# A grouped norm whose roots enter as factors per token in the projection's sums

## The chip, the core and the metric

The kernel runs on one core of a Trainium2 chip. Its time is the device time of one execution in microseconds. Before the change the runs took 817.53 us (median of 3, 816.61 to 818.11).

A core has five engines that work side by side and meet through semaphores. TensorE (PE in the profile, its weight loads PEld) multiplies matrices out of SBUF into the eight banks of PSUM. VectorE (DVE) and ScalarE (ACT) work element by element on SBUF and PSUM. GpSimd (POOL) works on SBUF, and SyncE (SP) issues the loads. Each engine takes its own instructions in a fixed order.

## The reference, cut to what matters

Two layers, 256 tokens, width 1024, all float32. In each layer three branches (a Mamba-2 scan, a sliding-window attention, a forgetting attention) are fed by one input projection, gated, projected, and merged. The scan branch ends in a norm over four groups of 256 channels, and then comes its projection:

```python
def grouped_rms_norm(y, w, groups):
    b, s, d = y.shape
    yf = y.astype(jnp.float32).reshape(b, s, groups, d // groups)
    yf = yf * lax.rsqrt(jnp.mean(yf * yf, axis=-1, keepdims=True) + NORM_EPS)
    return (yf.reshape(b, s, d) * w.astype(jnp.float32)).astype(y.dtype)

# mamba2_branch ends in:
    y = y.reshape(b, s, SSM_INNER) * jax.nn.silu(z)
    return grouped_rms_norm(y, norm_w, SSM_GROUPS)

# and in each layer:
        ys = jnp.stack([y_a, y_b, y_c], axis=2)
        branch = jnp.einsum('bsiw,iwd->bsid', ys, w_proj[layer])
        g = jax.nn.sigmoid(gates.reshape(b, s, N_BRANCH, d) + gate_bias[layer])
        merged = jnp.sum(g * branch, axis=2)
        x = x + jnp.einsum('bsd,de->bse', merged, w_out[layer])
```

For each token and each group there is one root. It multiplies 256 channels of that token, and all of them lie in the sum over `w` of the projection. So a root can be applied before the projection, to each channel, or behind it, to the part of the sum that belongs to its group.

## The kernel before

**Precision.** A float32 operand is split into a high part, rounded to the format that TensorE takes at full rate (fp32r), and the low rest. A product of two operands is three matmuls, high by high, low by high and high by low. `split` (L288) makes the two parts: ScalarE rounds (`hi`, L291) and VectorE subtracts (`lo`, L292).

**Weights.** They come in by DMA as raw parts of 512 KB, six buffers, and are split into `hi` and `lo` parts of 128x1024, six buffers each. A piece of 512 output columns has four parts, each with two of the eight blocks of 128 input channels (`k`). `feed` (L384) issues the next split when a part is given back by `release` (L404), behind the last matmul that reads it. A piece is worked on once for each of the two token blocks of 128 (`t`), so its parts are given back in the second token block.

**Order.** TensorE's order is written out by the program: `ops` is a list of pieces of weights with the work on each. Smaller steps (the attentions, the scan, the norm) are generators started by `launch` (L113) with a due time in a clock that counts matmul time. `pump` (L148), called within and after the pieces, enters those that are due; `drain` (L163) forces all steps with a given number. `finish` (L847) hangs queued work of the other engines (`ends_later`) behind a given instruction of ScalarE. The order of VectorE, ScalarE and POOL is laid out by the planner that compiles the program, by program order, readiness and the buffers that are free; `high_priority` puts instructions ahead.

**The scan branch's end** in each layer is this list: four pieces of 256 columns for the gate path (`u_z` with `br == 0`, two channel blocks `u` of 128 each), two gate pieces of 512 of the scan branch, one gate piece of the third branch, then the projection of the scan branch in two pieces of 512, then the rest of the third branch.

`u_z` multiplies the scan's output `y.xs` by the gate path (`normed`), squares it on ScalarE and adds the squares of two blocks, which make a group. `group_norm` (L953) is launched for each of the four groups. It sums the squares over the channels by matmuls against ones, so that each token is a partition (L955). POOL takes the power -1/2 (L961), and VectorE refines it by a Newton step (L966 to L969). The roots must then multiply a layout in which channels are partitions and tokens run along a row. So a root's high and low parts are put on diagonals of 128x128 (ScalarE, L976), and a matmul of a matrix of ones by the diagonals copies them to all partitions (two matmuls of 256 columns into PSUM). VectorE multiplies `y.xs`, the norm's weight and this broadcast (L989), and the result is split into `y.yh[0]` and `y.yl[0]`, the left operands of the projection.

**The projection** of the first piece is `u_proj2` with `tok2`: two PSUM banks, one for each token block, and the halves of `k` in turn (t0, t1, t0, t1). The second piece is `u_proj`, one token block after the other, 24 matmuls into one bank. `merge` (L1111) multiplies the gate and the bank's sum (VectorE, L1118) and adds to the merged sums on POOL (L1119).

**PSUM** has three banks tagged "mm" (`pmm`) for dense products and five tagged "mx" (`pmx`) for everything else. Other buffers that the change touches: `L1` (14, one row of 256 floats), `L2` (8, 512 floats) and `L8` (6, 2048 floats).

Of the kernel before, what the change touches and what calls it, by code (L numbers as in the profile page):

```python
# [11 lines left out]
F32 = mybir.dt.float32  # L12
F32R = mybir.dt.float32r
# [35 lines left out]
def hybrid_trunk(  # L49
# [17 lines left out]
    def T(tag, shape, dtype=F32, bufs=None):  # L67
        count[0] += 1
        return sb.tile(shape, dtype, tag=tag, name=f"{tag}_{count[0]}",
                       bufs=bufs if bufs is not None else BUFS.get(tag, 1))  # L70
# [8 lines left out]
    def pmx():  # L79
        return PS("mx", 5)  # L80
# [20 lines left out]
    def mm(o, a, b, **kw):  # L101
        n = b.free_size()
        if a.dtype == F32R:
            clock["t"] += max(0.094, n / 2350.0)
        else:
            clock["t"] += max(0.2, n / 587.0) * (0.5 if a.free_size() == 64 or a.shape[0] == 32 else 1.0)
        nc.tensor.matmul(o, a, b, **kw)  # L107
# [5 lines left out]
    def launch(br, gen, delay=0.0):  # L113
        clock["n"] += 1
        waiting.append([clock["t"] + delay, clock["n"], br, gen, None, False])
# [32 lines left out]
    def pump(budget=BUDGET):  # L148
        t0 = clock["t"]
        half = False  # L150
        while True:
            over = clock["t"] - t0 >= budget
            if over and not half:
                return
            for m in sorted(waiting, key=lambda m: (m[0], m[1])):
                if ready(m) and (m[5] if over else not early(m)):
                    half = m[5]
                    enter(m)
                    break
            else:  # L160
                return

    def drain(br):  # L163

        left = 0
        while any(m[2] == br for m in waiting):
            for m in sorted(waiting, key=lambda m: (m[0], m[1])):
                if m[2] == br and allowed(m):
                    left += 1
                    enter(m)  # L170
                    break
            else:
                m = min((m for m in waiting if allowed(m)), key=lambda m: (m[0], m[1]))
                left += 1
                enter(m)
        if left and VERBOSE:
            print("drained", br, left, "at", round(clock["t"], 1))
# [103 lines left out]
    def halves(ap):  # L281

        return ap.rearrange("p (a i) -> p a i", a=2)
# [4 lines left out]
    def split(hi, lo, src, scale=None, keep=lambda f: f):  # L288

        if scale is None:  # L290
            keep(act)(hi, src, AF.Copy)  # L291
            keep(tt)(lo, src, hi.bitcast(F32), op=ALU.subtract)  # L292
        else:
            keep(act)(hi, src, AF.Copy, scale=scale)
            keep(stt)(lo, src, scale, hi.bitcast(F32), op0=ALU.mult, op1=ALU.subtract)
# [618 lines left out]
    def u_z(y, br, u, c):  # L914
        def f(w):
            if u == 0 and br != 0:
                y.sz[br] = T("L8", [P, NK, S])
            elif u == 0:
                y.yh[br] = T("L8", [P, 2, NK, P], F32R)
                y.yl[br] = T("L8", [P, 2, NK, P], F32R)  # L920
            o = T("L1", [P, S]) if br == 0 else y.sz[br][:, u, :]

            def gated():
                th = T("L1", [P, S])
                act(th, o, AF.Tanh, scale=0.5)  # L925
                stt(o, th, 1.0, o, op0=ALU.add, op1=ALU.mult)
                y.zdone.add((br, u))
            if br == 1:
                dma_sum(y, w, c, o)
                after_evictions(3, gated)  # L930
                pump()
                return
            chan_sum(y, w, c, o)

            def normed():
                gated()
                tt(y.xs[:, u, :], y.xs[:, u, :], o, op=ALU.mult)
                sq = T("L1", [P, S])
                act(sq, y.xs[:, u, :], AF.Square)
                y.sq.append(sq)  # L940
                if u % 2 == 1:
                    tt(y.sq[-2], y.sq[-2], y.sq[-1], op=ALU.add)
                    launch(3 if u < 4 else 4, group_norm(y, u // 2, y.sq[-2]), D_GN1)
            if br == 0:
                drain(0)

                ends_later.append(normed)
            else:
                gated()
            pump()  # L950
        return f

    def group_norm(y, g, q0):  # L953
        p = pmx()
        for t in range(2):  # L955
            mm(p[:, 2 * t:2 * t + 2], q0[:, t * P:(t + 1) * P], ones[:, 0:2], start=True, stop=True)
        v = T("sm", [P, 8])
        ts(v[:, 0:4], p[:, 0:4], 1.0 / 256, 4 * EPS, op0=ALU.mult, op1=ALU.add)  # L958

        r0 = T("sm", [P, 8])  # L960
        nc.gpsimd.tensor_tensor(r0[:, 0:4], v[:, 0:4], mhalf[:, 0:4], op=ALU.pow)  # L961
        rbs = [T("L1", [P, S], F32R) for _ in range(2)]

        def diagonals():
            a = T("sm", [P, 8])
            tt(a[:, 0:4], r0[:, 0:4], v[:, 0:4], op=ALU.mult)  # L966
            tt(a[:, 0:4], a[:, 0:4], r0[:, 0:4], op=ALU.mult)
            r = T("rs", [P, 8], bufs=4)
            stt(r[:, 0:4], a[:, 0:4], -3.0, r0[:, 0:4], op0=ALU.add, op1=ALU.mult)  # L969

            rh, rl = T("sm", [P, 8], F32R), T("sm", [P, 8])
            nc.vector.tensor_copy(rh[:, 0:4], r[:, 0:4])
            tt(rl[:, 0:4], r[:, 0:4], rh[:, 0:4].bitcast(F32), op=ALU.subtract)
            for rb, v_ in zip(rbs, (rh.bitcast(F32), rl)):
                for t in range(2):
                    act(rb[:, t * P:(t + 1) * P], ident, AF.Copy, scale=v_[:, 2 * t:2 * t + 1])  # L976


        ends_later.append(diagonals)
        yield D_GN2  # L980
        if diagonals in ends_later:
            ends_later.remove(diagonals)
            diagonals()
        p = pmx()
        for i, rb in enumerate(rbs):
            mm(p[:, 0:S], onesr, rb, start=(i == 0), stop=(i == 1))
        for u in (2 * g, 2 * g + 1):
            n = T("L1", [P, S])
            stt(n, y.xs[:, u, :], y.vec[:, 80 + u:81 + u], p[:, 0:S], op0=ALU.mult, op1=ALU.mult)  # L989
            split(y.yh[0][:, :, u, :], y.yl[0][:, :, u, :], halves(n))  # L990


    def u_cv(y, c, t, i=None):
# [85 lines left out]
    def u_proj(y, br, c, t):  # L1079
        def f(w):  # L1080
            if c == 0 and t == 0:
                drain(3 if br == 0 else br)
                if br == 1:
                    y.mg = T("L8", [P, 2, D])
                if br == 2:
                    y.mh = T("L8", [P, 2, NK, P], F32R)
                    y.ml = T("L8", [P, 2, NK, P], F32R)
            final = br == 2 and c > 0 and t == 1
            if final:

                j = stream.index((pieces_out[y.l], 0)) + 2
                limit(j, False)
            merge(y, br, c, t, tok(y.yh[br], y.yl[br], w, t), pin if final else lambda f: f)
            if final:
                limit(j + 1, True)
            pump()
        return f

    def u_proj2(y, br):

        def f(w):
            def late():
                drain(4)
                pump()
            drain(3)
            for t, p in enumerate(tok2(y.yh[br], y.yl[br], w, (pump, late, pump, lambda: None))):
                merge(y, br, 0, t, p)
            pump()
        return f

# [137 lines left out]
    for y in layers:  # L1248
# [27 lines left out]
        def gates_proj(br):  # L1276
            def g(b):
                c = 512 * b
                op(cols(C_G + D * br + c, 512), u_gate(y, br, c, 0), u_gate(y, br, c, 1))

            def p(b):
                c = 512 * b
                if b == 0 and br != 0:
                    op(None, lambda y=y: split_late(y, br))
                i = sub([(0, w_proj[l, br, :, c:c + 512])], 512)
                if b == 0 and br == 0:
                    op(i, u_proj2(y, br))
                else:
                    op(i, u_proj(y, br, c, 0), u_proj(y, br, c, 1))
            seq = [(g, 0), (p, 0), (g, 1), (p, 1)]  # L1290
            if br == 1 and l == 0:

                seq = [(g, 0), (g, 1), (p, 0), (p, 1)]
            if br == 0:

                seq = [(lambda b: z1(C_ZA, 0, b), b) for b in range(4)] + [(g, 0), (g, 1), (p, 0), (p, 1)]
            return [lambda f=f, b=b: f(b) for f, b in seq]
# [265 lines left out]
```

## Time and profile before

| | before |
|---|---|
| median of 3 runs | 817.53 us (816.61 to 818.11) |
| the profiled execution | 816.47 us, span 814.7 us |
| granted TensorE clock | 0.999 |
| TensorE, weight loads | 805.0 us, 717.2 us busy |
| VectorE, ScalarE, GpSimd | 675.2, 538.2, 162.6 us busy |
| HBM read | 154.63 MB, 192 GB/s over the span |

The span runs from the first to the last instruction of one execution. A row of the profile names engine, line, operation and tiles as "written<-read". L107 is the helper that issues every matmul, so its rows are told apart by tiles: `mm` and `mx` are the PSUM banks, `hi` and `lo` the weight parts, `L` any of the buffers `L1` to `L16`. "x4" counts instructions. A piece of the chain in order of time has a start, a length and what it was; an idle time in square brackets names what ended it. In the rows of matmuls the duration is that of a pipelined instruction, and the distance between two starts is what each costs.

### The profile page before, as it was taken

How to read it: one execution, taken by the hardware profiler on the slowest of the kernel's cores; microseconds unless marked ns; L12 is line 12 of the kernel's file. 1: busy time of each engine (PE TensorE's matmuls, PEld its weight loads, DVE VectorE, ACT ScalarE, POOL GpSimd, SP SyncE). 2: the span in 40 equal slices, each digit the busy share in tenths (PEclk: the TensorE clock that was granted, in tenths of full speed). 3: DMA queues.
4: the chain of work that ended last, by engine and by line, in shares of the span. 5: the costliest groups of instructions: out<-in, count | busy, mean ns of one | idle time of the engine just before them, and what ended most of it. 6: DMA issues, size and time to landing. Idle time of an engine off the chain costs nothing.

```text
span 814.7 us, 14971 instructions
## 1 busy us (share of the span) xinstructions
PE 805.0 (99%) x5198; PEld 717.2 (88%) x5198; DVE 675.2 (83%) x1452; ACT 538.2 (66%) x1168; POOL 162.6 (20%) x233
## 2 busy tenths in 40 slices
PE   9999999999999999999999999999999999999996
PEld 8998988888888988888999898888888889888896
DVE  6878899989998788865776989997989878787665
ACT  7777768865776768543666776885557767674452
POOL 3066113130310111130005711313002110102100
PEclk9999999999999999999999999999999999999999
DMA  9898787687865554866789878768877565467632
GB/s 316 279 258 197 220 225 203 195 251 227 234 208 181 156 165 146 270 200 205 235 261 265 198 219 226 198 199 237 247 234 205 153 190 169 133 210 261 206 104 77
DMA packets 138708, 170.35 MB, mean 209 GB/s; under 512 B 9346, under 2 KB 106362, under 8 KB 138634
## 3 DMA queue, kind: packets, MB, share of 16 engines
q1 hardware_dynamic: 114960, 140.53, 54.6%
q0 software_dynamic: 12928, 12.63, 9.6%
q10 hardware_dynamic: 10746, 16.24, 6.6%
q8 instruction: 41, 0.67, 0.3%
q14 instruction: 33, 0.27, 0.1%
HBM read 154.63 MB, written 2.16 MB: 192 GB/s over the span
## 4 chain that ended last, share of the span: by engine, by line
PE 81%; DVE 10%; DMA 3%; ACT 3%; issue 3%; ACTq 0%; DVEq 0%
PE mm L107 72%; PE mx L107 6%; PE mx L111 3%; DVE lo L292 3%; DMA L<-cumd 3%; DVE L L830 2%; ACT hi L291 1%; ACT pp L614 0%; DVE L L292 0%; ACT L L827 0%; DVE pp L643 0%; DVE L L894 0%; DMA L<-in_x_dram 0%; DVE pp L619 0%; DVE L L679 0%
## 5 line engine op out<-in xcount | busy, mean ns | idle before, releaser
L107 PE MATMUL mm<-L,hi 128*128 128x512 f32 x1056 | 355.3, 387 | 1.0 <-ACT qt L491 0.7
L292 DVE TENSOR_TENSOR lo<-raw,hi 128x1024 fp32r<-128x1024 f32 (+2 forms) x276 | 312.5, 1151 | 51.1 <-ACT hi L291 48.3
L107 PE MATMUL mm<-hi,L 128*128 128x512 f32 (+2 forms) x1232 | 322.9, 351 | 0.1
L291 ACT ACTIVATE hi<-raw 128x1024 fp32r<-128x1024 f32 (+2 forms) x276 | 265.0, 980 | 59.0 <-PE mm L107 49.3
L107 PE MATMUL mm<-L,lo 128*128 128x256 f32 x1056 | 266.6, 273 | 0.0
L107 PEld LDWEIGHTS mm<-hi,L 128*128 128x128 f32 x1232 | 217.3, 190 | 24.1 <-issue 1.3
L107 PEld LDWEIGHTS mm<-L,hi 128*128 128x128 f32 x1056 | 195.2, 190 | 29.0 <-issue 3.7
L107 PE MATMUL mm<-lo,L 128*128 128x512 f32 (+2 forms) x616 | 213.6, 348 | 0.0
L107 PEld LDWEIGHTS mm<-L,lo 128*128 128x128 f32 x1056 | 202.1, 191 | 5.2
L107 PEld LDWEIGHTS mm<-lo,L 128*128 128x128 f32 x616 | 116.3, 190 | 11.6
L492 POOL DMA_DIRECT2D L<-L x68 | 59.4, 885 | 193.0 <-ACT L L491 130.0
L830 DVE SCALAR_TENSOR_TENSOR L<-L,vec,L 128x255 f32<-128x255 f32 (+2 forms) x96 | 46.2, 481 | 1.7
L490 ACT ACTIVATE L<-mm 128x256 f32<-128x256 f32 x84 | 31.7, 378 | 21.0 <-PE mm L107 19.0
L1040 POOL TENSOR_SCALAR_AFFINE_SELECT bias<-bias 128x128 f32<-128x128 f32 x64 | 27.1, 459 | 87.1 <-DMA bias<-cumd 87.0
L1074 ACT ACTIVATE L<-L 128x512 f32<-128x512 f32 x24 | 15.1, 630 | 30.4 <-DVE L L1071 26.0
L656 ACT ACTIVATE pp<-pp,nm 128x128 f32<-128x128 f32 x64 | 28.2, 441 | 9.9 <-DVE nm L650 9.9
L492 POOL DMA_DIRECT2D qt<-L x16 | 13.8, 860 | 88.8 <-ACT qt L491 43.3
L614 ACT ACTIVATE pp<-pp,nm 128x128 f32<-128x128 f32 x32 | 12.6, 394 | 23.5 <-DVE nm L619 22.7
L961 POOL TENSOR_TENSOR sm<-sm,mhalf 128x4 f32<-128x4 f32 x8 | 9.9, 1240 | 88.2 <-DVE sm L958 88.2
L925 ACT ACTIVATE L<-L 128x256 f32<-128x256 f32 x48 | 19.8, 412 | 10.2 <-DVE L L483 10.0
L491 ACT ACTIVATE L<-mm 128x256 f32<-128x256 f32 x68 | 25.9, 381 | 0.7 <-DMA L<-L 0.7
L1119 POOL TENSOR_TENSOR L<-L,L 128x512 f32<-128x512 f32 x8 | 12.8, 1595 | 67.1 <-DVE L L1118 67.1
(210 smaller groups left out, 872.7 us busy)
## 6 DMA issues: line engine op xcount, KB each, us to landing
raw<-in_w_in_dram SPq DMA_DIRECT2D x191, 512.0 KB, 4.8
raw<-in_w_proj_dram SPq DMA_DIRECT2D x48, 512.0 KB, 5.4
L<-L POOLq DMA_DIRECT2D x72, 128.0 KB, 4.8
raw<-in_w_out_dram SPq DMA_DIRECT2D x16, 512.0 KB, 5.0
bias<-cumd ACTq DMA_DIRECT2D x16, 256.0 KB, 3.4
L<-cumd ACTq DMA_DIRECT2D x8, 512.0 KB, 6.0
L<-in_gate_bias_dram ACTq DMA_DIRECT2D x12, 256.0 KB, 5.0
qt<-L POOLq DMA_DIRECT2D x16, 128.0 KB, 5.5
```

The lines of the kernel that those rows point to most:

```text
L107: nc.tensor.matmul(o, a, b, **kw)
L111: nc.tensor.transpose(o, a, i)
L291: keep(act)(hi, src, AF.Copy)
L292: keep(tt)(lo, src, hi.bitcast(F32), op=ALU.subtract)
L490: act(halves(lo), ordered(p[:, S:2 * S]), AF.Copy)
L491: last = act(halves(out), ordered(p[:, 0:S]), AF.Copy)
L492: nc.gpsimd.dma_start(out, lo, accum_op=ALU.add)
L656: act(pp[:, i, sl], pp[:, i, sl], AF.Exp, scale=-1.0, bias=nm[:, e:e + 1], accum_out=sums[:, e:e + 1])
L830: stt(a[:, s:S], x_[:, 0:S - s], y.vec[:, 16 * j + u:16 * j + u + 1], a[:, s:S], op0=ALU.mult, op1=ALU.add)
L925: act(th, o, AF.Tanh, scale=0.5)
L1040: nc.gpsimd.affine_select(out=bias[:, i, dst], in_=bias[:, i, src], compare_op=ALU.is_ge, fill=NEG, base=0, pattern=[[-1, P]], channel_mul ...
L1074: finish(act(g, g, AF.Tanh, scale=0.5))
```

## The change

The roots are no longer applied to the channels. In `u_z` each block is split as soon as it is gated, with the norm's weight as the factor and without the root. The four groups' sums of squares are taken in one step (`group_norms`), launched after the last block: eight matmuls against ones into one bank, one evaluation and one power for all eight columns (group by token block), and one Newton step, queued in `ends_later`. The roots stay as they come, one token per partition.

Both projection pieces go through `u_proj_normed`: for each token block four sums of six matmuls, one per group, in banks taken in turn from "mm" and "mx". ScalarE copies the first with the root as its scale, and VectorE multiplies each of the other three by its root and adds. The merge then reads the result from SBUF. The diagonals, the broadcast matmuls and the multiplication by the broadcast go. `u_proj2` goes with them.

```diff
@@ u_z
             def normed():
                 gated()
                 tt(y.xs[:, u, :], y.xs[:, u, :], o, op=ALU.mult)
+                split(y.yh[0][:, :, u, :], y.yl[0][:, :, u, :], halves(y.xs[:, u, :]), scale=y.vec[:, 80 + u:81 + u])
                 sq = T("L1", [P, S])
                 act(sq, y.xs[:, u, :], AF.Square)
                 y.sq.append(sq)
                 if u % 2 == 1:
                     tt(y.sq[-2], y.sq[-2], y.sq[-1], op=ALU.add)
-                    launch(3 if u < 4 else 4, group_norm(y, u // 2, y.sq[-2]), D_GN1)
+                if u == NK - 1:
+                    launch(3, group_norms(y, y.sq[0::2]), D_GN1)
...
-    def group_norm(y, g, q0):
...
+    def group_norms(y, squares):
         p = pmx()
+        for g, q in enumerate(squares):
+            for t in range(2):
+                c = 4 * g + 2 * t
+                mm(p[:, c:c + 2], q[:, t * P:(t + 1) * P], ones[:, 0:2], start=True, stop=True)
+        v, r0 = T("sm", [P, 8]), T("sm", [P, 8])
+        ts(v, p[:, 0:16].rearrange("p (g i) -> p g i", i=2)[:, :, 0], 1.0 / 256, 4 * EPS, op0=ALU.mult, op1=ALU.add)
+        gtt(r0, v, mhalf, op=ALU.pow)
+
+        def newton():
+            y.roots = T("rs", [P, 8], bufs=4)
+            tt(v, r0, v, op=ALU.mult)
+            tt(v, v, r0, op=ALU.mult)
+            stt(y.roots, v, -3.0, r0, op0=ALU.add, op1=ALU.mult)
+
+        ends_later.append(newton)
+        yield 0.0
+
+    def u_proj_normed(y, c, t):
+        def f(w):
+            if c == 0 and t == 0:
+                drain(3)
+                for _ in range(len(ends_later)):
+                    ends_later.pop(0)()
+            acc = T("L2", [P, 512])
+            for g in range(4):
+                p = (pmx if g % 2 else pmm)()
+                for k in (2 * g, 2 * g + 1):
+                    for i, (a, b) in enumerate(((y.yh[0], w.hi), (y.yl[0], w.hi), (y.yh[0], w.lo))):
+                        mm(p, a[:, t, k, :], in_turn(b(k)), start=(k == 2 * g and i == 0),
+                           stop=(k == 2 * g + 1 and i == 2))
+                    if w.last and (k + 1) % w.kper == 0:
+                        release(w, k // w.kper + 1)
+                r = y.roots[:, 2 * g + t:2 * g + t + 1]
+                with tc.high_priority():
+                    if g == 0:
+                        act(acc, p, AF.Copy, scale=r)
+                    else:
+                        stt(acc, p, r, acc, op0=ALU.mult, op1=ALU.add)
+                if g == 1:
+                    pump()
+            merge(y, 0, c, t, ordered(acc))
+            pump()
+        return f
...
-    def u_proj2(y, br):
...
@@ gates_proj
-                if b == 0 and br == 0:
-                    op(i, u_proj2(y, br))
+                if br == 0:
+                    op(i, u_proj_normed(y, c, 0), u_proj_normed(y, c, 1))
```

More of the change, by code (lines that the diff above doesn't have):

```diff
@@ L951, in u_z @@
         return f
-    def group_norm(y, g, q0):
+    def group_norms(y, squares):
         p = pmx()
[L955 to L990, printed above, removed]
@@ L1081, in f @@
             if c == 0 and t == 0:
-                drain(3 if br == 0 else br)
+                drain(br)
                 if br == 1:
@@ L1095, in f @@
                 limit(j + 1, True)
-            pump()
-        return f
-    def u_proj2(y, br):
[L1101 to L1107, printed above, removed]
             pump()
```

## The prediction

> **What bounds the kernel now.** I read the page first: shares of the engines, and the chain that ended last.
>
> ```profile
> PE 805.0 (99%) x5198; PEld 717.2 (88%) x5198; DVE 675.2 (83%) x1452; ACT 538.2 (66%) x1168; POOL 162.6 (20%) x233
> ...
> PE 81%; DVE 10%; DMA 3%; ACT 3%; issue 3%; ACTq 0%; DVEq 0%
> ```
>
> TensorE is busy almost throughout and holds 81% of the chain; a fifth of the chain is elsewhere. So the stretch that the change touches has to be read alone. The chain in order of time shows it, first for layer 1 and then for layer 0 (start, length, what):
>
> ```profile
> 706.26 0.24 PE mx L107 x2
> 706.50 7.77 PE mm L107 x36
> 714.27 0.34 PE mx L107 x4
> 714.61 2.70 PE mm L107 x12
> 717.31 0.47 PE mx L107 x4
> 717.78 10.36 PE mm L107 x48
> 728.14 0.23 PE mx L107 x2
> 728.37 31.73 PE mm L107 x147
> ```
>
> ```profile
> 305.02 0.68 PE mx L107 x6
> 305.71 5.18 PE mm L107 x24
> 310.89 0.24 PE mx L107 x2
> ...
> 319.35 0.24 PE mx L107 x2
> ...
> 329.94 0.24 PE mx L107 x2
> ```
>
> The reader is to see that nothing but TensorE stands in the chain here: each piece starts where the one before it ends. The "mx" pieces are the norm's own: x4 are the sums of squares of a group (four matmuls against ones), x2 the broadcast of its roots. 48 large matmuls take 10.36 us, 0.216 each: one piece of 512 columns, two token blocks. The table by stage shows who stands behind TensorE (columns: PE, weight loads, DVE, ACT, POOL, each busy us and count, then granted clock, DMA share, GB/s). The four stretches are gates and projection of the scan branch in layer 0, then in layer 1:
>
> ```profile
> 296.00:332.00 36.00, 36.00 (x199) 31.19 (x197) 28.45 (x60) 26.84 (x53) 3.87 (x3) 1.00 0.58 176
> 332.00:353.00 21.00, 21.00 (x99) 18.40 (x98) 15.91 (x19) 8.97 (x10) 4.69 (x3) 1.00 0.71 219
> 700.00:733.00 33.00, 33.00 (x163) 29.19 (x164) 27.22 (x61) 23.52 (x47) 3.00 (x3) 1.00 0.55 168
> 733.00:754.00 21.00, 21.00 (x99) 18.40 (x98) 15.31 (x17) 10.21 (x11) 4.67 (x3) 1.00 0.77 259
> ```
>
> The clock is full, VectorE has 5 to 8 us free in each stretch. A microsecond of matmul taken out here comes off the end, as long as VectorE and ScalarE go on delivering the split weights in time.
>
> **What TensorE loses.** Per group two broadcast matmuls go, 16 in all. Their steps in the chain: 0.24 + 0.47 (two pairs) + 0.23 = 0.94 us in layer 1; in layer 0 three of 0.24, and of the x6 piece what is over the 0.34 of a x4 piece, 0.34: 1.06. Sum 2.0 us. The timeline gives the same for one pair by its starts: 310.96 - 310.72 = 0.24.
>
> ```profile
> 310.72 0.40 PE L107 MATMUL mx<-L,ones 128*128 128x256 f32 x2
> 310.96 0.60 PE L107 MATMUL mm<-hi,L 128*128 128x512 f32 x2
> ```
>
> The sums of squares stay 32 matmuls, but in one block per layer instead of four. What that is worth lies between 0.5 us saved and 0.5 us lost (a quarter of 0.34 for each of the six blocks that no longer stand apart); I take 0, since the nearest row is the same matmul. The projection's matmuls stay 96 of 512 columns per layer, now as four sums of six. Each sum begins on another PSUM bank with a wait for its reader. Between the two token blocks of a piece the same happens today inside the unbroken 31.73 us of 147 steps (0.216 each), so I price it at 0 while a bank is free: the sums alternate between three "mm" and five "mx" banks, each is filled in 1.3 us, and so a "mm" bank is asked for again some 6 us after its sum is complete. Without that cover each late reader would cost TensorE its lateness.
>
> **What the other engines lose and gain.** Rows of layer 0, grouped by line over gates and projection, VectorE and then ScalarE (last columns: busy us, mean ns of one, idle before):
>
> ```profile
> L989 DVE SCALAR_TENSOR_TENSOR L<-L,vec,mx 128x256 f32<-128x256 f32 x8 | 3.5, 475 | 0.5 <-PE mx L107 0.5
> L292 DVE TENSOR_TENSOR L<-L,L 128x256 fp32r<-128x256 f32 x8 | 3.1, 419 | 0.0
> L1118 DVE SCALAR_TENSOR_TENSOR L<-L,mm 128x512 f32<-128x512 f32 x4 | 2.7, 684 | 2.9 <-PE mm L107 2.9
> ...
> L966 DVE TENSOR_TENSOR sm<-sm,sm 128x4 f32<-128x4 f32 x4 | 0.6, 162 | 1.4 <-POOL sm L961 1.2
> ```
>
> ```profile
> L976 ACT ACTIVATE L<-ident,sm 128x128 fp32r<-128x128 f32 x16 | 5.1, 387 | 0.0
> ...
> L291 ACT ACTIVATE L<-L 128x256 fp32r<-128x256 f32 x8 | 3.0, 405 | 0.9 <-DVE L L989 0.9
> ...
> L696 ACT ACTIVATE L<-mx 128x512 f32<-128x512 f32 x3 | 1.7, 585 | 0.0
> ```
>
> Per layer VectorE loses 8 scalings (3.5 us) and of the small ones (six a group, 0.16 each) 24 become 4: 3.2 us. Its 8 subtractions of the split (3.1 us; now with a factor, about the same) move ahead of the gates, among the four channel pieces. ScalarE loses 16 diagonals (5.1 us), and 8 roundings (3.0 us) move with the subtractions. POOL has one power instead of four. The steps that move or go issue no DMA, so no queue of SP, ACT or POOL is passed by one. Added in the projection: per piece and token block one copy on ScalarE (585 ns is the nearest row) and three multiply-adds on VectorE (684 ns, the row of the same shape that reads PSUM); per layer 2.3 us and 12 x 0.684 = 8.2 us. The merge stays and reads SBUF instead of PSUM: by the 128x256 rows here 475 from PSUM, 419 for a two-input SBUF instruction, so no dearer; I take it as equal.
>
> So the gate stretch is relieved by 3.5 + 3.1 + 3.2 = 9.8 us of VectorE and some 8 of ScalarE, and the projection has 8.2 more: 15.91 + 8.2 = 24.1 us in 21 (23.3 without the last two subtractions of the old norm), in layer 1 23.5. VectorE is then full for two pieces and falls some 2.5 us behind. What covers that is the lead of the split weights. The last of the four weight parts in the following piece (layer 0): both subtractions of the row end at 353.03, its first matmul starts at 357.64.
>
> ```profile
> 350.56 2.47 DVE L292 TENSOR_TENSOR lo<-raw,hi 128x1024 fp32r<-128x1024 f32 x2 [1.53 <-ACT hi L291]
> ...
> 357.64 0.38 PE L107 MATMUL mm<-lo,L 128*128 128x512 f32 x1
> ```
>
> 4.6 us of lead against 2.5 behind: no stall, cost 0; without the lead those 2.5 us would come on top in each layer. The first piece also changes from two half blocks in turn to one token block after the other, so its first weights are released 2.6 us later; the lead of 4.6 is measured at pieces that already go that way.
>
> In the channel pieces the 3.1 us move in before the gates. There the lead is longer: the first gate part is done at 287.82 and used at 297.16.
>
> ```profile
> 286.60 1.22 DVE L292 TENSOR_TENSOR lo<-raw,hi 128x1024 fp32r<-128x1024 f32 x1
> ...
> 297.16 0.38 PE L107 MATMUL mm<-lo,L 128*128 128x512 f32 x1
> ```
>
> The new wait is the Newton step's for POOL's power: once a layer, up to 1.2 us by the row of L966, with a gate's eviction and a subtraction behind it, instead of four such waits. The scaled halves are written earlier, so their two large buffers are taken some 35 us earlier; at that point the stream's values, the merged sums, the last attention's values and its gate path hold four of the six, which just fits. The squares of four groups are held until the one block, four of 14 small buffers.
>
> **The sum.** -2.0 (broadcast) + 0 (sums of squares) + 0 (banks) + 0 (VectorE) = -2.0 us. The profiled execution took 816.47 us, 1.06 below the median of the runs, so 814.5 on its scale and 817.53 - 2.0 = 815.5 on that of the median.
>
> One rule would lower this. The Trainium skill (Perfetto Trace Analysis, Identifying the Most-Contended Engine) says that matmul occupancy is no good measure of TensorE and that the busy share of weight loads is one. By that share, 18.40 of 21.00 us or 88%, TensorE has an eighth free, and the gain would be 0.88 x 2.0 = 1.8, or 815.7. The unbroken 0.216 us steps decide for 2.0; both lie in the forecast's own range.
>
> **The rivals.** First, *no change that counts*. About 0.2% (1.6 us) is what a measurement of this kernel can tell from no change, and 2.0 is little over it. The order of VectorE and ScalarE is laid out anew by the planner, and in layer 1's convolution stage the chain is not TensorE's:
>
> ```profile
> 553.47 7.60 DMA L<-cumd
> ```
>
> Half a microsecond lost there leaves -1.5 and 816.0; 1 us gives 816.5. For it: such a transfer starts when work on other engines is done. Against it: that stage lies before the change in its layer, and delays are counted from the layer's own work. That the broadcast was hidden anyway is out, since it stands in the chain.
>
> Second, *slower: the gate pieces run out of split weights*. The last part of the third gate piece is done at 726.64 and used at 727.11 in layer 1, a lead of 0.5 us, and in layer 0 at 324.37 and 326.33, 2.0 us:
>
> ```profile
> 725.42 1.22 DVE L292 TENSOR_TENSOR lo<-raw,hi 128x1024 fp32r<-128x1024 f32 x1
> ...
> 727.11 0.38 PE L107 MATMUL mm<-lo,L 128*128 128x512 f32 x1
> ```
>
> ```profile
> 323.15 1.22 DVE L292 TENSOR_TENSOR lo<-raw,hi 128x1024 fp32r<-128x1024 f32 x1
> ...
> 326.33 0.38 PE L107 MATMUL mm<-lo,L 128*128 128x512 f32 x1
> ```
>
> If the work put in front arrives there as lateness, that is 3.1 us, or 6.3 if VectorE, which takes its instructions in order, also waits for each of the 8 roundings (0.405). I take 3.1, as a rounding needs only its own channel's product and can be done while VectorE subtracts. TensorE then waits 2.6 + 1.1 = 3.7 us: 815.5 + 3.7 = 819.2, just over the border. It decides from 0.5 us of lateness on. For it speaks the thin lead, against it that 9.8 us leave just this stretch.
>
> Third, *slower: the projection's evictions*. VectorE falls more than 4.6 us behind and both the banks and the weights come late. By load alone it is 2.5 us. If each of the four merges of a layer also waited out an addition on POOL (1.28 us), 2.5 + 5.1 - 4.6 = 3.0 us a layer: 821.5.
>
> ```profile
> 341.83 1.28 POOL L1119 TENSOR_TENSOR L<-L,L 128x512 f32<-128x512 f32 x1 [24.71 <-DVE L L1118]
> ...
> 342.80 1.39 DVE L292 TENSOR_TENSOR lo<-raw,hi 128x1024 fp32r<-128x1024 f32 x1 [1.11 <-ACT hi L291]
> ...
> 344.93 2.13 POOL L1119 TENSOR_TENSOR L<-L,L 128x512 f32<-128x512 f32 x1 [1.82 <-DVE L L1118]
> ```
>
> Such meetings show today: the subtraction that meets an addition takes 1.39 instead of 1.22, another addition 2.13 instead of 1.28. But merges come 5 us apart, and the addition is over by then. The Trainium skill (SBUF — State Buffer, Who interferes with whom) has the rule: a VectorE instruction with two SBUF inputs and a GpSimd one that reads SBUF exclude each other, and the merge now has two. These rows agree in kind.
>
> **How the numbers follow.** Forecast, -2.0 with at most 0.4 given back: 0.53, all of it faster. No change that counts: 0.26 (816.5). Gate pieces: 0.14 (819.2). Evictions: 0.07 (821.5). So faster 0.53, same 0.26, slower 0.21. Range: down to 814.0 (0.5 from the sums of squares and 1.0 from a lucky order where TensorE is off the chain), up to 819.6, which takes in the gate rival and leaves the evictions out. The forecast's own range is 814.5 to 815.9.
>
> **What would show it.** In the changed profile the x2 "mx" pieces are gone and one "mx" piece of 16 stands in the gates of each layer; the steps in the projection stay 0.216 us through all four sums; multiply-adds of 128x512 number 24 at about 0.68; VectorE is at 9 to 10 tenths in the projection and lower in the gates; the third gate piece's last part leads by more than 2 us. Wrong it would be if TensorE has gaps at a sum's first matmul (banks) or at a part's first (weights), or if the gain is there at the end of layer 0 and gone at layer 1's gates.

## The result, and the profile after

The changed kernel took 815.33 us (median of 8 runs, 814.85 to 816.26) against 816.99 us (8 runs, 815.78 to 818.11) of the kernel before on the same chip: a ratio of 0.9978, interval 0.9969 to 0.9987, or 1.8 us less (1.1 to 2.5); the two medians are 1.66 apart. The profiled execution took 815.95 us, with a span of 814.2 us and a granted clock of 0.998.

The page of the changed kernel, engines and the chain that ended last:

```profile
PE 803.2 (99%) x5182; PEld 714.8 (88%) x5182; DVE 684.4 (84%) x1420; ACT 534.4 (66%) x1144; POOL 157.4 (19%) x227
...
PE 88%; DVE 4%; DMA 4%; ACT 2%; issue 2%; SPq 0%; DVEq 0%; ACTq 0%
```

TensorE has 1.8 us less to do and 16 matmuls fewer, VectorE 9.2 us more. The chain in order of time, first layer 0 (start, length, what):

```profile
313.57 1.68 PE mx L107 x16
315.25 19.53 PE mm L107 x90
334.78 1.29 PE mx L107 x6
336.08 1.29 PE mm L107 x6
```

and layer 1, up to the last of the four-part sums:

```profile
701.31 14.45 PE mm L107 x76
715.76 1.68 PE mx L107 x16
717.44 16.94 PE mm L107 x78
734.38 1.29 PE mx L107 x6
735.68 1.29 PE mm L107 x6
...
752.51 1.29 PE mx L107 x6
753.81 10.36 PE mm L107 x48
```

The pieces of two "mx" matmuls are gone. The sums of squares are one piece of 16 steps. In the projection each sum of six matmuls takes 1.29 us, 0.216 a step, and each begins where the one before it ended: no bank was waited for. The long pieces behind the block of squares (x90, x78) are the gates; they run through too.

The table by stage, for the same four stretches as before (gates and projection of layer 0, then of layer 1):

```profile
296.00:332.00 36.00, 36.00 (x199) 31.23 (x198) 26.35 (x43) 22.20 (x36) 2.06 (x1) 1.00 0.64 201
332.00:353.00 21.00, 21.00 (x99) 18.40 (x99) 19.55 (x22) 11.61 (x14) 3.44 (x3) 1.00 0.64 202
700.00:733.00 33.00, 33.00 (x181) 28.75 (x178) 23.98 (x37) 19.22 (x30) 1.69 (x1) 1.00 0.57 192
733.00:754.00 21.00, 21.00 (x99) 18.42 (x98) 19.92 (x23) 11.81 (x15) 4.70 (x3) 1.00 0.69 215
```

VectorE (third pair of numbers) went from 15.91 to 19.55 and from 15.31 to 19.92 us in the projections, and fell in the gates from 28.45 to 26.35 and from 27.22 to 23.98. The gain can be placed by setting the same matmul's start in one profile beside its start in the other. At 200 us the changed kernel was 1.62 us later than the kernel before (a difference between two executions, far ahead of the change: two later runs of the kernel before with small edits behind this point lag the same profile by 1.71 and 1.50 us there), at 333 us 0.71: a gain of 0.91 us in layer 0. In layer 1 it went from 0.43 later at 590 us to 0.47 earlier at 733.8: 0.90. Between 333 and 590 us the lag moves between 0.92 and 0.43, and behind 733.8 it stays: nothing was given back.

The new work, by line, on VectorE and ScalarE in gates and projection of layer 0 (last columns: busy us, mean ns of one, idle before):

```profile
L998 DVE SCALAR_TENSOR_TENSOR L<-mx,rs,L 128x512 f32<-128x512 f32 x7 | 5.2, 742 | 0.6 <-PE mx L107 0.5
L295 DVE SCALAR_TENSOR_TENSOR L<-L,vec,L 128x256 fp32r<-128x256 f32 x6 | 2.9, 478 | 0.6 <-ACT L L294 0.6
L1119 DVE SCALAR_TENSOR_TENSOR L<-L,L 128x512 f32<-128x512 f32 x3 | 2.5, 823 | 0.1
...
L996 ACT ACTIVATE L<-mm,rs 128x512 f32<-128x512 f32 x4 | 2.7, 679 | 0.8 <-PE mm L107 0.8
L294 ACT ACTIVATE L<-L,vec 128x256 fp32r<-128x256 f32 x5 | 2.5, 508 | 2.5 <-DVE L L937 2.5
```

L998 is the multiply-add, L295 and L294 the split with the norm's weight as a factor, L1119 the merge, L996 the copy with the root as its scale. All five are dearer than the rows that they were priced by.

### The profile page after: what moved, and what is told of

It reads as the page before. It is cut to its first block, busy times and chain, and to the rows that moved or that the text cites. A ratio compares the mean times of both kernels' runs of the same rounds, so it can differ in the third digit from the quotient of the medians.

```text
span 814.2 us, 14891 instructions
## 1 busy us (share of the span) xinstructions
PE 803.2 (99%) x5182; PEld 714.8 (88%) x5182; DVE 684.4 (84%) x1420; ACT 534.4 (66%) x1144; POOL 157.4 (19%) x227
## 4 chain that ended last, share of the span: by engine, by line
PE 88%; DVE 4%; DMA 4%; ACT 2%; issue 2%; SPq 0%; DVEq 0%; ACTq 0%
PE mm L107 76%; PE mx L107 9%; PE mx L111 3%; DMA L<-cumd 3%; DVE lo L292 2%; DVE L L830 1%; DMA raw<-in_w_in_dram 1%; DVE L L292 0%; ACT L L827 0%; DVE L L894 0%; ACT hi L291 0%; DVE L L879 0%; DVE L L1084 0%; ACT L L881 0%; ACT L L1087 0%
## 5 line engine op out<-in xcount | busy, mean ns | idle before, releaser
L292 DVE TENSOR_TENSOR lo<-raw,hi 128x1024 fp32r<-128x1024 f32 (+2 forms) x276 | 313.9, 1157 | 46.1 <-ACT hi L291 44.3
L107 PE MATMUL mm<-hi,L 128*128 128x512 f32 (+2 forms) x1168 | 303.8, 349 | 0.1
L107 PEld LDWEIGHTS mm<-hi,L 128*128 128x128 f32 x1168 | 206.0, 190 | 22.5 <-issue 1.3
L107 PE MATMUL mm<-lo,L 128*128 128x512 f32 (+2 forms) x584 | 201.6, 347 | 0.0
L107 PEld LDWEIGHTS mm<-lo,L 128*128 128x128 f32 x584 | 110.4, 190 | 10.6
L1053 POOL TENSOR_SCALAR_AFFINE_SELECT bias<-bias 128x128 f32<-128x128 f32 x64 | 29.0, 488 | 86.2 <-DMA bias<-cumd 60.7
L614 ACT ACTIVATE pp<-pp,nm 128x128 f32<-128x128 f32 x32 | 12.6, 394 | 24.9 <-DVE nm L619 24.1
L925 ACT ACTIVATE L<-L 128x256 f32<-128x256 f32 x48 | 19.7, 411 | 9.7 <-DVE L L483 9.5
L836 ACT ACTIVATE L<-L 128x256 f32<-128x256 f32 x32 | 13.4, 418 | 17.8 <-DVE L L830 17.6
```

Source lines behind the costliest of these rows:

```text
L1053: nc.gpsimd.affine_select(out=bias[:, i, dst], in_=bias[:, i, src], compare_op=ALU.is_ge, fill=NEG, base=0, pattern=[[-1, P]], channel_mul ...
```

## The experiments

**The broadcasts put back, read by nobody.** Eight matmuls of the broadcast's size in each layer, behind the sums of squares:

```diff
+        for g in range(4):
+            pb = pmx()
+            for i in range(2):
+                mm(pb[:, 0:S], onesr, y.yh[0][:, 0, 0:2, :], start=(i == 0), stop=(i == 1))
```

> The changed kernel with eight matmuls of 256 columns put back into each layer, right behind the sums of squares, as a broadcast would need them; nobody reads what they write. All else is as changed. Theory (the gain is TensorE's time for the broadcast): 0.12 us each, 16 of them, so 1.9 us come back and the time is that of the kernel before, ratio 1.000 (0.999 to 1.001). Rival (the gain came from the relief of VectorE and ScalarE in the gates, or from a luckier order of the other engines): the matmuls cost less than 0.7 us and the ratio stays below 0.9987.

Measured: 817.31 us (11 runs, 816.41 to 818.66) against 817.49, ratio 0.9999 (0.999 to 1.0008). The chain has the eight in the block:

```profile
313.65 2.74 PE mx L107 x24
...
716.11 2.74 PE mx L107 x24
```

2.74 against 1.68 is 1.06 us more a layer in the chain, and the gain is gone. Beside the changed kernel's, the starts of the same matmuls behind the block move by 0.95 us in each layer, 1.90 for the 16; the other 0.1 is a tail that the chain otherwise puts into the next piece. So it was the broadcast matmuls on TensorE that the change saved; all that it saves and adds on the other engines makes, together, no difference that these runs can tell.

**The four sums alone.** The kernel before, with its norm, its diagonals and its broadcast, and only the projection in four sums with a factor of one (so the result stays the same):

```diff
+    def u_proj_four(y, c, t):
...
+                r = ones[:, 0:1]
...
-                if b == 0 and br == 0:
-                    op(i, u_proj2(y, br))
+                if br == 0:
+                    op(i, u_proj_four(y, c, 0), u_proj_four(y, c, 1))
```

> The kernel before with only the projection of the change: four sums per token block in banks in turn, added up by ScalarE and VectorE with a factor of one, while the roots still come in through the broadcast. Theory (VectorE's 8.2 us more per layer hide behind the lead of the split weights): ratio 1.000, between 0.999 and 1.001, no gap of TensorE in the projection. Rival (the evictions cost something that the changed kernel pays for out of the relieved gates): here nothing is relieved, VectorE enters the projection with the old norm's last work, and 1 to 6 us are lost, ratio 1.001 to 1.008.

Measured: 817.3 us (11 runs, 816.62 to 818.04), ratio 0.9995 (0.9987 to 1.0004). The two projections in the table by stage:

```profile
332.00:353.00 21.00, 21.00 (x99) 18.40 (x98) 21.00 (x28) 11.60 (x16) 3.41 (x2) 1.00 0.71 212
733.00:754.00 21.00, 21.00 (x99) 18.40 (x98) 20.83 (x26) 12.50 (x17) 3.41 (x2) 1.00 0.85 262
```

VectorE is busy all the time and TensorE does not stop. The leads of the following piece's last weights fall to 1.5 us in layer 0 and 2.2 us in layer 1, and hold. The added evictions are hidden even where the gates ahead of them were not relieved.

**Each multiply-add twice.** The changed kernel, with a second copy of every multiply-add whose result is not used:

```diff
+                        junk = T("L2", [P, 512])
+                        stt(junk, p, r, acc, op0=ALU.mult, op1=ALU.add)
                         stt(acc, p, r, acc, op0=ALU.mult, op1=ALU.add)
```

> The changed kernel with each multiply-add of the projection made twice, the first time into a buffer that nobody reads: 12 more of 0.74 us in each layer. VectorE then has some 32 us of work in 21 us of the projection. Theory (the lead of the weights is all that covers): it falls 2.5 + 8.9 = 11.4 us behind against a lead of 4.6, so TensorE waits up to 6.8 us a layer; time 820 to 829, with gaps at a sum's first matmul or at a part's first. Rival (VectorE has room that the sum of busy times does not show): less than 2 us lost.

Measured: 825.08 us (5 runs, 822.41 to 825.41), ratio 1.0087 (1.0071 to 1.0102): 9.75 us over the changed kernel's median, which was taken in another set of runs. In the profiles the same matmuls start 4.7 us later across layer 0's projection and what follows it, and 3.9 in layer 1. The same 12 x 0.742 = 8.9 us a layer that cost nothing the first time cost about half of that the second. The waits around layer 0's projection (who waited for whom: us, times, longest) and the table by stage:

```profile
PEld mm L107 <- DVE L L1000: 3.2, 2, 1.9
PE mm L107 <- DVE L L1000: 2.4, 2, 1.5
```

```profile
332.00:356.00 24.00, 22.09 (x102) 18.68 (x100) 23.48 (x28) 11.53 (x14) 3.41 (x2) 1.00 0.61 189
733.00:758.00 25.00, 24.14 (x112) 20.83 (x111) 22.84 (x27) 13.53 (x16) 2.48 (x2) 1.00 0.63 194
```

In the projection TensorE now waits for banks which the multiply-add (L1000 here) has not read yet: the starts move by 3.0 us in layer 0 and 2.9 in layer 1. Behind the projection they move by 1.8 and 1.0 more, and there TensorE waits for the split weights (1.4 and 0.8 us for the `lo` parts of L292). So this is the stop that the prediction named as its third rival, banks and weights both, and the load at which it comes lies between one and two multiply-adds a sum.

**One multiply-add in three twice.** To bring that load nearer, the same second copy only for the second sum, four a layer:

```diff
+                        if g == 1:
+                            junk = T("L2", [P, 512])
+                            stt(junk, p, r, acc, op0=ALU.mult, op1=ALU.add)
                         stt(acc, p, r, acc, op0=ALU.mult, op1=ALU.add)
```

> The changed kernel with one multiply-add more per token block of the projection, into a buffer that nobody reads: 4 more of 0.74 us in each layer, 3.0 us. In the changed kernel the least lead behind the projection is 2.4 to 3.0 us. Theory (the lead is a store that is used up before anything is lost): at the border, 0 to 0.6 us lost per layer, ratio to the kernel before 0.997 to 0.9995. Rival (each microsecond of VectorE in the projection costs its share, as 8.9 us cost 4.9 per layer): 1.6 us per layer, 3.3 in all, ratio 1.002.

Measured: 816.29 us (11 runs, 815.4 to 819.93) against 817.13, ratio 0.9992 (0.9982 to 1.0003), so 1.1 us of the change's 1.8 is lost if the middles are taken, and the interval does not exclude that nothing is. By the starts of the same matmuls 0.4 us are lost in each layer, behind the projection. In the timeline the last weight part of the following piece in layer 1 ends just before it is read:

```profile
755.83 1.96 DVE L292 TENSOR_TENSOR lo<-raw,hi 128x1024 fp32r<-128x1024 f32 x1
...
757.92 0.40 PE L107 MATMUL mm<-lo,L 128*128 128x512 f32 x1
```

755.83 + 1.96 = 757.79, used at 757.92: 0.1 us of lead where the changed kernel has 3.0. About three microseconds of VectorE a layer (4 x 0.742) are what the projection can still take, as the theory had it.

**One broadcast matmul instead of two.** The kernel before with the broadcast of the roots' high part alone; the low part is left out of the result. This takes away half of the supposed gain and adds nothing:

```diff
-            for rb, v_ in zip(rbs, (rh.bitcast(F32), rl)):
+            for rb, v_ in zip(rbs[:1], (rh.bitcast(F32),)):
...
-        for i, rb in enumerate(rbs):
-            mm(p[:, 0:S], onesr, rb, start=(i == 0), stop=(i == 1))
+        mm(p[:, 0:S], onesr, rbs[0], start=True, stop=True)
```

> The kernel before with the high part of the roots alone on the diagonals: one broadcast matmul per group instead of two, half the diagonals on ScalarE, and no subtraction for the low part, which is left out. Theory (TensorE's time for the broadcast is the gain): 8 matmuls of 0.12 us less, -0.95 us, ratio 0.9988 (0.998 to 0.9995), half of what the change gave. Rival (the gain hangs on the waits of the norm's chain or on the early split, which stay here): ratio 1.000.

Measured: 816.6 us (11 runs, 815.28 to 817.75), ratio 0.9992 (0.9983 to 1.0001). The chain has 0.12 us where there were 0.24:

```profile
312.26 0.12 PE mx L107
...
706.71 0.12 PE mx L107
```

Over the stretch (275 to 333 us in layer 0, 690 to 740 in layer 1) the starts of the same matmuls gain 0.48 us in layer 0 and 0.46 in layer 1, the four times 0.12 that were taken out. By the runs' times alone a gain is not shown, since the interval reaches past 1; size and direction fit a gain of half.

**The squares summed at full rate.** The changed kernel with the squares rounded to fp32r ahead of the sum over channels, which makes each of the eight matmuls one step instead of two; the sums lose the low part of the squares:

```diff
-                    tt(y.sq[-2], y.sq[-2], y.sq[-1], op=ALU.add)
+                    q = T("L1", [P, S], F32R)
+                    tt(q, y.sq[-2], y.sq[-1], op=ALU.add)
+                    y.sq[-2] = q
...
-                mm(p[:, c:c + 2], q[:, t * P:(t + 1) * P], ones[:, 0:2], start=True, stop=True)
+                mm(p[:, c:c + 2], q[:, t * P:(t + 1) * P], onesr[:, 0:2], start=True, stop=True)
```

> The changed kernel with the squares of a group rounded to fp32r when they are added, so that the sums over channels are single matmuls at full rate: 8 instead of 16 per layer. The rounding of the squares is what it gives up. Theory (TensorE's chain is the time in this stretch): the block of 1.68 us in each layer becomes about 0.85, so 1.7 us less than the changed kernel, 813.6; ratio to the kernel before 0.996. Rival (a microsecond off this stretch comes back elsewhere): ratio stays 0.998.

Measured: 814.08 us (5 runs, 812.93 to 814.32), ratio 0.9956 (0.9943 to 0.9968). The block in the chain:

```profile
312.71 0.79 PE mx L107 x8
...
715.06 0.79 PE mx L107 x8
```

0.79 instead of 1.68, 0.9 us in each layer, and the starts behind the block come 0.89 us earlier in each: again as it stands in the chain. This kernel is faster than both, at the price of the squares' low part.

**VectorE loaded in the channel pieces.** The prediction moved eight subtractions a layer ahead of the gates and covered them by the long lead of the weights there. Here each is made three times, 16 x 0.48 = 7.7 us of VectorE more a layer; the two further results are not used:

```diff
-                split(y.yh[0][:, :, u, :], y.yl[0][:, :, u, :], halves(y.xs[:, u, :]), scale=y.vec[:, 80 + u:81 + u])
+                hi_, lo_, w_ = y.yh[0][:, :, u, :], y.yl[0][:, :, u, :], y.vec[:, 80 + u:81 + u]
+                act(hi_, halves(y.xs[:, u, :]), AF.Copy, scale=w_)
+                for _ in range(2):
+                    junk = T("L1", [P, S])
+                    stt(halves(junk), halves(y.xs[:, u, :]), w_, hi_.bitcast(F32), op0=ALU.mult, op1=ALU.subtract)
+                stt(lo_, halves(y.xs[:, u, :]), w_, hi_.bitcast(F32), op0=ALU.mult, op1=ALU.subtract)
```

> The changed kernel with the split's subtraction in the channel pieces made three times instead of once, twice into a buffer that nobody reads: 16 more of 0.48 us in each layer, 7.7 us of VectorE ahead of the gates. Theory (the leads there are 4 to 12 us in the changed kernel and VectorE has 9 us free in the gates): less than 1 us lost, ratio to the kernel before between 0.997 and 0.9995. Rival of the prediction (lateness from the channel pieces reaches the gate pieces): more than 2 us lost, ratio above 1.000, with waits of TensorE at a weight part of the second or third gate piece.

Measured: 821.01 us (5 runs, 820.31 to 822.92), ratio 1.0041 (1.0028 to 1.0055): 5.7 us over the changed kernel. The expectation of less than 1 us was wrong. The channel pieces of layers 0 and 1 in the table by stage, first of the changed kernel, then of this one (whose layer 1 lies 4 us later):

```profile
276.00:300.00 24.00, 24.00 (x155) 21.60 (x154) 21.45 (x59) 20.50 (x51) 0.00 (x0) 1.00 0.56 160
...
680.00:705.00 25.00, 25.00 (x165) 22.08 (x164) 24.21 (x65) 20.29 (x54) 0.00 (x0) 1.00 0.61 177
```

```profile
276.00:300.00 24.00, 22.63 (x146) 19.95 (x145) 21.57 (x62) 19.49 (x47) 0.00 (x0) 1.00 0.51 146
...
680.00:705.00 25.00, 23.31 (x147) 20.33 (x146) 23.45 (x65) 20.55 (x49) 0.00 (x0) 1.00 0.58 168
```

TensorE has gaps there. The split weights were not late: their leads stay at 2.6 us and more. The waits of layer 1's channel pieces and layer 0's chain at the gap name another store:

```profile
PE mm L107 <- DVE L L483: 2.1, 4, 0.9
```

```profile
293.40 1.14 DVE lo L292
294.54 0.34 DVE L L926
294.88 0.07 DVE L L483
...
298.54 0.34 DVE L L483
298.88 0.14 issue
299.01 4.99 PE mm L107 x22
```

L483 is the addition that reads a channel sum out of its "mm" bank and gives it back. It queues on VectorE behind other work, and TensorE waits for the bank. In the profiled execution (822.92 us, the longest of the five) the starts of the same matmuls lose 1.85 us around layer 0's channel pieces and 3.0 around layer 1's; the waits for these banks reach into the first gate piece, and none is for a `lo` part. So the rival had the size right and the wait wrong. Some 1.8 us more were lost in layer 1 ahead of this, where a transfer in the chain (`cumd`) took 5.32 us and in the changed kernel 3.64; why, these runs do not show. So the subtractions that the change moved were hidden, but not by what the prediction said. VectorE is busy for 24.21 of 25 us there in the changed kernel.

**Columns put in order while PSUM is read.** TensorE writes the columns of a piece's two halves in turn (0, 256, 1, 257 and so on). The changed kernel copies and adds them as they lie, and the merge reads the sum out of SBUF with a step of two. Here the copy and the multiply-adds read PSUM with a step of two, so that the merge reads its sum in order; the squares are summed at full rate as above:

```diff
-                        act(acc, p, AF.Copy, scale=r)
+                        act(halves(acc), ordered(p), AF.Copy, scale=r)
...
-                        stt(acc, p, r, acc, op0=ALU.mult, op1=ALU.add)
+                        stt(halves(acc), ordered(p), r, halves(acc), op0=ALU.mult, op1=ALU.add)
...
-            merge(y, 0, c, t, ordered(acc))
+            merge(y, 0, c, t, halves(acc))
```

> The kernel with the sums of squares at full rate, and the columns put in order as the banks are read (by the copy and the multiply-adds) instead of by the merge, which then reads SBUF in order. The rounding of the squares is what it gives up. Theory: the merge's 0.83 us fall to about 0.69 since its second SBUF input no longer steps over every other element, the multiply-adds stay at 0.74, and as VectorE is hidden there the time stays at 814.1, ratio 0.995 to 0.9965. Rival (the merge is slow because it has two SBUF inputs): it stays at 0.83.

Measured: 813.34 us (5 runs, 813.21 to 814.1), ratio 0.9953 (0.994 to 0.9965). The merge of the changed kernel, then merge and multiply-add of this one (durations in ns: lowest, median, highest):

```profile
L1119 DVE SCALAR_TENSOR_TENSOR L<-L,L x8: 805/830/849, 339.5 to 758.5; 128x512 f32<-128x512 f32 x8
```

```profile
L1121 DVE SCALAR_TENSOR_TENSOR L<-L,L x8: 676/692/693, 337.7 to 755.4; 128x512 f32<-128x512 f32 x8
```

```profile
L1000 DVE SCALAR_TENSOR_TENSOR L<-mx,rs,L x16: 737/746/753, 334.4 to 753.6; 128x512 f32<-128x512 f32 x16
```

The merge falls from 830 to 692 ns, and the multiply-add stays (742 and 746). It is the step of two in SBUF that made the merge dear. The time is within the interval of the kernel with the full-rate sums alone: a microsecond of VectorE that was hidden is worth nothing measurable. By its median it is the fastest version that was run.

**The multiply-add with a constant factor.**

```diff
-                        stt(acc, p, r, acc, op0=ALU.mult, op1=ALU.add)
+                        stt(acc, p, 1.0, acc, op0=ALU.mult, op1=ALU.add)
```

> The changed kernel with the constant 1.0 as the factor of the 24 multiply-adds in place of the per-token root; the roots of groups 1 to 3 are so left out of the result, and the work is otherwise the same. Theory: a factor that is a column of the on-chip memory costs VectorE about 60 ns an instruction (478 ns against 419 for 128x256 in the changed kernel's rows), so the multiply-add's row falls from 742 to about 684 ns. Rival: the second operand, the accumulator in the on-chip memory, is what makes the step long, and the row stays at 742. The time: within 0.3% of the changed kernel under both, about 0.998 of the kernel before, since the projection's evictions are hidden.

Measured: 814.93 us in one run, beside 816.07 for the kernel before, so 0.9986. The row:

```profile
L998 DVE SCALAR_TENSOR_TENSOR L<-mx,L x16: 677/682/727, 335.9 to 755.4; 128x512 f32<-128x512 f32 x16
```

682 ns against 742: the factor that lies in SBUF, one value per partition, costs 60 ns an instruction. It accounts for the whole difference from the 684 ns of the row by which the multiply-add was priced.

## Why the prediction was right, step by step

**The broadcast, -2.0.** The sign and the mechanism held. Putting the matmuls back takes the whole gain away, halving them gives about half, and the starts move by 0.91 and 0.90 us, 1.81 together. That the time of 815.33 us lies so near the 815.5 of the forecast is in part luck: the kernel before took 816.99 us here and not the 817.53 that the forecast started from, and the gain was smaller by 0.2 to 0.3 us. The term was read a tenth too large in layer 0. The prediction split the piece of six (0.68) into 0.34 for the squares and 0.34 for the pair. A block of squares has a tail of 0.11 that the chain puts into the next piece: 12 matmuls behind one take 2.70 us where 12 x 0.216 make 2.59. The 24 behind the piece of six take 5.18, which is 24 x 0.216, so there the tail lies inside: 0.45 and 0.24. Four pairs of 0.24 are 0.96 in layer 0, and the sum is 1.9.

**Sums of squares, 0.** Four blocks of 0.34 with 0.11 behind each are 1.8 us; the one block is 1.68, and the 78 matmuls behind it take 16.94 where 78 x 0.216 make 16.85, so 1.8 too. The value taken was right, because a step costs 0.11 us with the tail, in one block as in four. What could be saved there is the second step of each matmul, 0.9 us a layer, as the run at full rate shows.

**Banks, 0.** Right: no piece in the projection is longer than 1.30, and it takes twice the multiply-adds to make TensorE wait for a bank.

**VectorE, 0.** Right in the cost, wrong in the sizes. The multiply-add was taken as 684 ns and is 742; the merge was taken as equal and went from 684 to 830; the copy on ScalarE was taken as 585 and is 679. On VectorE that is 12 x 0.058 + 4 x 0.146 = 1.3 us a layer more than expected. What failed is the reading of the 128x256 rows: 475 against 419 was put down to PSUM, and with it the merge out of SBUF was to be no dearer. The row of 475 also had the norm's weight, a factor per partition, and the run with a constant factor shows, at 128x512, that such a factor costs 60 ns. The split's subtraction shows it at 128x256: 419 without the factor, 478 with it, which the prediction took as about the same. For ScalarE the Trainium skill (ScalarE: Activation LUTs, What ACT_TABLE_LOAD costs) states the price: each operand of one value per partition adds about 93 ns. 585 + 93 = 678, and the row here is 679: it agrees, by rows of two lines. For the merge, the Trainium skill (SBUF — State Buffer, Door 1: The DMA port swizzle) lets a float32 operand be read with gaps at no cost as long as two reads fall into a line of 16 bytes, which a step of two does; the 830 against 692 ns speak against it for this instruction, and the measurement decides.

Against that stood a relief that was not counted. VectorE was to need 24.1 us in layer 0's projection and was busy for 19.55 of 21. Three of the twelve multiply-adds (2.2 us) fell behind this stretch. And its splits of activations there before the change were these, by form:

```profile
L292 DVE TENSOR_TENSOR L<-L,L 128x512 fp32r<-128x512 f32 x4 | 2.6, 684 | 0.0
L292 DVE TENSOR_TENSOR L<-L,L 128x256 fp32r<-128x256 f32 x2 | 0.8, 418 | 0.0
```

The prediction took out the 0.8. In the changed kernel the other four are done before the projection as well; its rows by form from 290 to 332 us have them:

```profile
L292 DVE TENSOR_TENSOR L<-L,L 128x512 fp32r<-128x512 f32 x4 | 2.7, 686 | 0.0
```

So in layer 0 the relieved gates took 2.6 us of work out of the projection. The relief itself was smaller than the 9.8 us of the prediction: the table by stage has 2.1 and 3.2 us less of VectorE in the gates, where these splits now stand, and four of the eight moved subtractions in layer 0 (1.9 us) and three in layer 1 (1.4 us) too. Where the gates keep the old norm, in the run with the four sums alone, VectorE is full (21.00 of 21.00), as the prediction had it. The lead of the last weights behind layer 0's projection fell from 4.6 to 3.0 us: 1.6 us of it were used, not 2.5.

**The channel pieces, 0.** Right in the cost, wrong in the cover. The prediction hid the moved subtractions behind the lead of the weights, 9 us. With three times the subtractions the weights are still in time, and the "mm" banks are not.

**POOL's power.** The wait was to be up to 1.2 us once a layer and is 1.58 in layer 0 and 1.80 in layer 1:

```profile
719.45 0.17 DVE L969 TENSOR_TENSOR sm<-sm,sm 128x8 f32<-128x8 f32 x1 [1.80 <-POOL sm L965]
```

It is hidden all the same: the gate weights behind it have 4 us to spare, as the next rows show.

**The rivals.** *Gate pieces run out of split weights*: it went the other way. In layer 1 the last part of the third gate piece is the second of these three subtractions, done at 722.3 and used at 726.88, 4.5 us later instead of 0.5:

```profile
719.96 3.66 DVE L292 TENSOR_TENSOR lo<-raw,hi 128x1024 fp32r<-128x1024 f32 x3
...
726.88 0.38 PE L107 MATMUL mm<-lo,L 128*128 128x512 f32 x1
```

The relief of VectorE in the gates reached the weights as lead, and nothing of the work put in front of them arrived as lateness. *Evictions*: they decide from about 3 us of VectorE more a layer, and at 8.9 more they cost 3.9 to 4.7. Merges that each waited out an addition on POOL were not seen (805 to 849 ns, all eight). *No change that counts*: the chance of it was real, as -1.8 with an interval from -2.5 to -1.1 lies just over what a measurement tells. Nothing was lost in layer 1's convolution stage; the changed kernel keeps layer 0's gain through it (0.87 us later at 535 us, 0.43 at 590).

That 0.88 of the term would be gained instead of all of it (1.8 for 2.0) is not decided by the runs' times, whose interval holds both. The chain is the better witness: 1.81 of the 1.9 that stood in it were gained, and the 16 matmuls put back moved the starts by 1.90, where 0.88 of 1.9 would be 1.7.

## What to carry to other kernels

Where the chain is TensorE's step after step, a few short matmuls are worth their distance from start to start, also when VectorE gets 9 us more to do, and that distance is read with the tail in the piece behind. For work moved onto VectorE ask for each stretch which store is used up first: in one stretch here it was the split weights (3 us left), in another the three PSUM banks, whose reader queued behind the new work (less than 7.7 us left). When a row is used as a price, its operands have to be the same too: a factor per partition (60 ns) and a step of two (138 ns) cost something here, while one input out of PSUM instead of SBUF made no difference that shows (682 against 692 ns for 128x512).

## What the runs showed of the hardware

A factor that is one value per partition in SBUF costs VectorE 60 ns an instruction (742 against 682 ns for 128x512) and, by rows of two lines, ScalarE 94 (679 against 585 for 128x512) and 103 (508 against 405 for 128x256). Reading SBUF with a step of two costs VectorE 138 ns for 128x512 (830 against 692); reading PSUM so costs nothing that shows (746 against 742). A float32 matmul against two columns takes two steps of 0.105 us (1.68 us for 16); the fp32r form takes one (0.79 us for eight). A subtraction of 128x1024 that meets an addition on POOL (from 340.45 on, 1.28 us) takes 1.90 us in place of 1.22:

```profile
340.92 1.90 DVE L292 TENSOR_TENSOR lo<-raw,hi 128x1024 fp32r<-128x1024 f32 x1 [0.61 <-ACT hi L291]
```

The prediction showed the milder case of it, 1.39.
